# Indexer and attention scores of a hybrid decoder trunk: from fp32 to three fp32r passes, two head groups in turn on the two halves of the partitions

## The chip, the cores and the metric

The kernel runs on one core of a Trainium2 chip. The metric is the device time of one execution in microseconds. Five engines work side by side: TensorE (PE, with its weight loads listed as PEld), VectorE (DVE), ScalarE (ACT), GpSimd (POOL) and SyncE (SP), which here only issues DMAs.

## What is computed

Two layers of a causal decoder trunk on 256 tokens of width 1024. Each layer has a half-step SwiGLU, a mixer with three branches (sparse attention, causal pooling, a chunked state-space scan), a second half-step SwiGLU and an input embedding. The change touches only the sparse attention: an indexer of 8 heads of 64 picks 64 keys per query, and 8 heads of 64 attend to them.

```python
idx = jnp.einsum("bqh,bqhs->bqs", wi,
                 jax.nn.relu(jnp.einsum("bqhd,bsd->bqhs", qi, k_idx)))
idx = jnp.where(causal[None], idx.astype(jnp.float32), -jnp.inf)
_, sel = lax.top_k(idx, k_top)
...
logits = jnp.einsum("bqhr,bqkr->bqhk", ql, c_sel).astype(jnp.float32) * (HEAD_DIM ** -0.5)
probs = jax.nn.softmax(logits, axis=-1).astype(c_sel.dtype)
```

All inputs are float32. The kernel doesn't gather: it computes the scores of all keys from `q` and `kt` (the keys in head space) and adds a mask to those that weren't chosen.

## The kernel before

Activations lie with channels on the partitions and 256 tokens in the free dimension. Weights come from memory in units of 128x1024 (SP queue, `load`), and each unit is split: ACT rounds it to fp32r (`whi`, L128), DVE takes what is left (`wlo`, L129). A dense product is then three fp32r passes, high by high, high by low and low by high (`mm3`, L151 to L153), each a matmul of 128x128 weights over 256 columns. `AHEAD` lets two units be loaded beyond the one in use; four buffers stand for `raw`, `whi` and `wlo`.

The two products that the change touches were plain fp32. `indexer` (L636) and `attention` (L679) go over the queries in two blocks of 128 (h = 0 with 128 keys, h = 1 with 256 keys). Two heads share a chunk of 128 partitions: even heads on partitions 0 to 63, odd heads on 64 to 127. A group (`heads`) is four heads (h = 0) or two heads (h = 1) of the same parity, so that its scores fill one PSUM bank of 512 columns; all its matmuls have 64 rows, on the same half. A group's scores then go to ACT (relu, L639) and DVE (L646) in the indexer, or to DVE (L686), ACT (exp, L688), transposes (L697) and the product with the values (L711) in attention. An fp32 matmul is two matmul instructions, each with its own weight load; a transpose and an fp32r matmul are one.

`mix` runs the branches as generators, `weave` takes steps from them in turn, and a scheduler under the tile layer then sets the order on each engine by its own estimate of times. `choose` (the indexer) runs beside `silus` (convolution, gate and query projections), `attend` beside `states`, `pools` and `gate`. So bursts of a few score matmuls stand between long rows of `mm3` passes. There are eight PSUM banks, four tagged `mm` for the dense products and four tagged `aux` for everything else. The tag `a4` had four buffers of 4 KB a partition, taken in turn by the indexer's queries `qi`, the queries `q`, the keys `kt`, the values `vt` and the outputs of the scan.

Of the kernel before, what the change touches and what calls it, by code (L numbers as in the profile page):

```python
# [9 lines left out]
F = mybir.dt.float32  # L10
FR = mybir.dt.float32r
I32 = mybir.dt.int32
AF = mybir.ActivationFunctionType
OP = mybir.AluOpType
AX = mybir.AxisListType

P = 128
D = 1024
S = 256
# [45 lines left out]
class Builder:  # L65
# [191 lines left out]
    def constants(self):  # L257
        nc = self.nc
        c = self.const
        self.ident = c.tile([P, P], F, name="ident")  # L260
        self.ones = c.tile([P, P], F, name="ones")
        self.tri = c.tile([P, P], F, name="tri")
        self.up = c.tile([P, P], F, name="up")
        self.upr = c.tile([P, P], FR, name="upr")
        nc.gpsimd.memset(self.ones, 1.0)
        nc.gpsimd.affine_select(out=self.ident, in_=self.ones, pattern=[[-1, P]],
                                compare_op=OP.is_equal, fill=0.0, base=0, channel_multiplier=1)

        nc.gpsimd.affine_select(out=self.tri, in_=self.ones, pattern=[[1, P]],
                                compare_op=OP.is_ge, fill=0.0, base=0, channel_multiplier=-1)  # L270
        nc.gpsimd.affine_select(out=self.up, in_=self.ones, pattern=[[-1, P]],
                                compare_op=OP.is_gt, fill=0.0, base=0, channel_multiplier=1)
        nc.vector.tensor_copy(self.upr, self.up)
        self.onesr = c.tile([P, P], FR, name="onesr")
        nc.vector.tensor_copy(self.onesr, self.ones)

        warm = self.t([P, 1], tag="warm", bufs=1)
        nc.gpsimd.memset(warm, 0.0)
        nc.scalar.activation(warm, warm, AF.Tanh)
        self.cc = []  # L280
        for i in range(DEPTH):
            cc = c.tile([P, NCC], F, name=f"cc{i}")
            (nc.scalar, nc.gpsimd)[i].dma_start(cc, self.ins["cc"][i])
            self.cc.append(cc)

    def col(self, layer, name, i=0, n=1):
# [94 lines left out]
    def mix(self, layer, nxt):  # L381
        nc = self.nc
# [35 lines left out]
                                 accum_out=ss[:, 2 + h:3 + h])  # L418


        qi = self.a([P, 4, S], F, "a4", 4)
        for i in range(0, 4, 2):
            ps = self.in_pair(layer, T_QI + i, u0)
            self.later()
            nc.vector.tensor_tensor(qi[:, i:i + 2], ps, rb, op=OP.mult)


        self.uh = self.a([P, KD, S], FR, "uh", 2)
# [8 lines left out]


        xs = self.a([P, 8, S], F, "uh", 2)
        q = self.a([P, 4, S], F, "a4", 4)  # L440
        mb = [None, None]
        ki = self.a([P, S], F, "ki")
        ct = self.a([P, 2, 2, S], FR, "ct")

        def choose():
            v4 = self.t([P, 4], tag="v4", bufs=1)
            nc.vector.tensor_scalar(v4[:, :2], ss[:, :2], 1.0 / 256, EPS, op0=OP.mult, op1=OP.add)
            nc.vector.tensor_scalar(v4[:, 2:], ss[:, 2:], 1.0 / 64, EPS, op0=OP.mult, op1=OP.add)
            rk = self.t([P, 4], tag="rk", bufs=1)
            self.rsqrt(rk, v4, 4)  # L450
            for h in range(2):
                nc.vector.tensor_scalar(cn[:, h], cn[:, h], rk[:, h:h + 1], None, op0=OP.mult)
                nc.vector.tensor_scalar(ki2[:, h], sm[:, h, None, 8:72].to_broadcast([P, 2, 64]),
                                        rk[:, 2 + h:3 + h], None, op0=OP.mult)
            yield
            yield
            yield
            pk = self.bank("aux")
            for h in range(2):
                nc.tensor.transpose(pk[:, h * P:(h + 1) * P],  # L460
                                    ki2[:, h].rearrange("p a b -> p (a b)"), self.ident)
            nc.scalar.mul(ki, pk[:, :S], self.col(layer, "idx_k_norm"))
            yield
            yield
            mb[0] = yield from self.indexer(layer, 0, sm, qi, ki, idx[:, 0])
            pc = self.bank("aux")
            for c in range(2):
                for h in range(2):
                    nc.tensor.transpose(pc[:, c * S + h * P:c * S + (h + 1) * P],
                                        cn[:, h, c * P:(c + 1) * P], self.ident)  # L470
            for c in range(2):
                self.split_scaled(ct[:, 0, c], ct[:, 1, c], pc[:, c * S:(c + 1) * S],
                                  self.col(layer, "kv_norm", c))
            yield
            mb[1] = yield from self.indexer(layer, 1, sm, qi, ki, idx[:, 1])

        def silus():
# [12 lines left out]
            for i in range(0, 4, 2):  # L490
                ps = self.bank()
                yield from self.in_steps(layer, T_Q + i, u, ps)
                ps = ps.rearrange("p (a b) -> p a b", a=2)
                nc.scalar.mul(q[:, i:i + 2], ps, -0.125)


        def gates():
# [20 lines left out]
        res = {}  # L518

        def attend():  # L520
            kt = self.a([P, 4, S], F, "a4", 4)
            vt = self.a([P, 2, 512], F, "a4", 4)
            wk = self.unit(layer, U_KV, 1024)
            for i in range(0, 4, 2):
                ps = self.bank("aux")
                for j in range(2):
                    for c in range(2):
                        s = slice(c * 512 + (i + j) * P, c * 512 + (i + j + 1) * P)
                        self.mm3(ps[:, j * S:(j + 1) * S], (wk[0][:, s], wk[1][:, s]),
                                 (ct[:, 0, c], ct[:, 1, c]), c == 0, c == 1)  # L530
                nc.scalar.copy(kt[:, i:i + 2], ps.rearrange("p (a b) -> p a b", a=2))
                yield
            wv = self.unit(layer, U_KV + 1, 1024)
            for h in range(2):
# [84 lines left out]
    def heads(g, n):  # L619
# [2 lines left out]
        return ([g // 2 * 2 * n + 2 * j + odd for j in range(n)],  # L622
                slice(odd * 64, odd * 64 + 64))

    def indexer(self, layer, h, sm, qi, ki, idx):

        nc = self.nc
        nk = (h + 1) * P
        per = 512 // nk
        qs = slice(h * P, (h + 1) * P)  # L630
        for g in range(8 // per):
            heads, rows = self.heads(g, per)
            ps = self.bank("aux")
            for j, hd in enumerate(heads):
                c = hd // 2
                nc.tensor.matmul(ps[:, j * nk:(j + 1) * nk], qi[rows, c, qs], ki[rows, :nk],  # L636
                                 start=True, stop=True)
            t = self.t([P, 512])
            nc.scalar.activation(t, ps, AF.Relu)  # L639
            for j, hd in enumerate(heads):  # L640
# [24 lines left out]
    def attention(self, layer, h, mb, q, kt, vt, ya):  # L665
# [5 lines left out]
        qs = slice(h * P, (h + 1) * P)  # L671
        py = self.bank("aux")
        before = None
        for g in range(8 // per):
            heads, rows = self.heads(g, per)
            ps = self.bank("aux")
            for j, hd in enumerate(heads):
                c = hd // 2
                nc.tensor.matmul(ps[:, j * nk:(j + 1) * nk], q[rows, c, qs], kt[rows, c, :nk],  # L679
                                 start=True, stop=True)  # L680
            pr = self.t([P, per, nk])
            mx = self.t([P, per], tag="mx", bufs=2)
            sums = self.t([P, per], tag="sum", bufs=2)
# [34 lines left out]
    def ssd(self, layer, sm, xs, bc, cb, zs):  # L718
# [64 lines left out]
        for g in range(2):  # L783
# [50 lines left out]
            yield  # L834
            if g == 0:
                ysh, ysl = [], []
            ysh.append(self.a([P, 4, S], FR, "a4", 4))
            ysl.append(self.a([P, 4, S], FR, "a4", 4))
            for i in range(4):
                k = g * 4 + i  # L840
                nc.vector.tensor_tensor(y[:, k], y[:, k], zs[:, k], op=OP.mult)
# [228 lines left out]
def program(arrays):  # L1070

    order = None
    for last in (False, True):
        nc = bacc.Bacc("TRN2", target_bir_lowering=False, num_devices=1)
        ins = {k: nc.dram_tensor(f"in_{k}_dram", v.shape, F, kind="ExternalInput").ap()
               for k, v in arrays.items()}
        out = nc.dram_tensor("out_0_dram", (2, P, D), F, kind="ExternalOutput").ap()
# [13 lines left out]
```

## Time and profile before

| | us |
|---|---|
| median of 3 runs | 1355.15 (1353.79 to 1355.48) |
| the profiled execution, whole time | 1354.48 |
| its span, first to last instruction | 1352.8 |
| PE, weight loads, DVE, ACT busy in it | 1336.3, 1312.7, 1039.7, 745.0 |

Matmuls are pipelined: a matmul's listed duration (277 ns for 256 columns) is the time until its result stands, and the next one starts earlier than that. What a matmul costs in a row of matmuls is read from the distance of starts in the timeline. A row of the timeline merges neighbours of one line: it gives the start of the first, the time from there to the end of the last, and their count.

### The profile page before, as it was taken

How to read it: one execution, taken by the hardware profiler on the slowest of the kernel's cores; microseconds unless marked ns; L12 is line 12 of the kernel's file. 1: busy time of each engine (PE TensorE's matmuls, PEld its weight loads, DVE VectorE, ACT ScalarE, POOL GpSimd, SP SyncE). 2: the span in 40 equal slices, each digit the busy share in tenths (PEclk: the TensorE clock that was granted, in tenths of full speed). 3: DMA queues.
4: the chain of work that ended last, by engine and by line, in shares of the span. 5: the costliest groups of instructions: out<-in, count | busy, mean ns of one | idle time of the engine just before them, and what ended most of it. 6: DMA issues, size and time to landing. Idle time of an engine off the chain costs nothing.

```text
span 1352.8 us, 28288 instructions
## 1 busy us (share of the span) xinstructions
PE 1336.3 (99%) x11500; PEld 1312.7 (97%) x11500; DVE 1039.7 (77%) x1962; ACT 745.0 (55%) x1203; POOL 3.1 (0%) x14
## 2 busy tenths in 40 slices
PE   8999999999999999999999999999999999999997
PEld 7999999999899999999999999999989999999997
DVE  7777669877889787766887766797788887777666
ACT  5545456648654554544655444565576545545454
POOL 0000000000000000000000000000000000000000
PEclk9999999999999999999999999999999999999999
DMA  7666656554356666666566666565533666666661
GB/s 255 190 199 190 196 162 199 172 180 125 110 170 188 196 194 196 191 199 191 185 187 190 198 190 191 180 187 161 175 110 110 192 203 190 194 196 191 195 193 62
DMA packets 67714, 242.97 MB, mean 180 GB/s; under 512 B 7520, under 2 KB 7648, under 8 KB 67584
## 3 DMA queue, kind: packets, MB, share of 16 engines
q1 hardware_dynamic: 66816, 239.89, 57.3%
q8 instruction: 90, 1.47, 0.4%
q10 hardware_dynamic: 720, 1.16, 0.2%
q14 instruction: 40, 0.33, 0.1%
q0 software_dynamic: 48, 0.11, 0.0%
HBM read 240.09 MB, written 1.05 MB: 178 GB/s over the span
## 4 chain that ended last, share of the span: by engine, by line
PE 95%; DVE 3%; ACT 1%; issue 0%; DMA 0%; SPq 0%; DVEq 0%; ACTq 0%
PE mm L151 29%; PE mm L152 29%; PE mm L153 29%; DVE wlo L129 1%; PE aux L679 1%; PE aux L636 1%; PE aux L151 1%; PE aux L152 1%; PE aux L153 1%; PE aux L798 1%; PE aux L809 1%; PE aux L711 1%; PE aux L697 0%; ACT whi L128 0%; DMA h<-in_x_dram 0%
## 5 line engine op out<-in xcount | busy, mean ns | idle before, releaser
L128 ACT CAST whi<-raw 128x1024 fp32r<-128x1024 f32 (+1 forms) x457 | 476.4, 1045 | 507.6 <-issue 245.9
L151 PE MATMUL mm<-uh,whi 128*128 128x256 f32 x2560 | 713.3, 279 | 6.5 <-ACT whi L145 5.9
L129 DVE TENSOR_TENSOR wlo<-raw,whi 128x1024 fp32r<-128x1024 f32 (+1 forms) x457 | 554.5, 1215 | 214.0 <-ACT whi L128 210.8
L152 PE MATMUL mm<-ul,whi 128*128 128x256 f32 x2560 | 710.3, 278 | 0.2
L153 PE MATMUL mm<-uh,wlo 128*128 128x256 f32 x2560 | 709.4, 277 | 0.0
L151 PEld LDWEIGHTS mm<-uh,whi 128*128 128x128 f32 x2560 | 482.1, 188 | 13.2 <-ACT whi L145 5.9
L152 PEld LDWEIGHTS mm<-ul,whi 128*128 128x128 f32 x2560 | 482.4, 188 | 1.7 <-DVE ul L172 0.9
L153 PEld LDWEIGHTS mm<-uh,wlo 128*128 128x128 f32 x2560 | 482.2, 188 | 0.7 <-issue 0.3
L153 PE MATMUL mm<-gh,wlo 128*128 128x256 f32 x704 | 194.3, 276 | 0.0
L151 PE MATMUL mm<-gh,whi 128*128 128x256 f32 x704 | 194.3, 276 | 0.0
L152 PE MATMUL mm<-gl,whi 128*128 128x256 f32 x704 | 194.3, 276 | 0.0
L152 PEld LDWEIGHTS mm<-gl,whi 128*128 128x128 f32 x704 | 132.2, 188 | 0.0
L153 PEld LDWEIGHTS mm<-gh,wlo 128*128 128x128 f32 x704 | 132.2, 188 | 0.0
L151 PEld LDWEIGHTS mm<-gh,whi 128*128 128x128 f32 x704 | 132.2, 188 | 0.0
L151 PE MATMUL mm<-a,whi 128*128 128x256 f32 x256 | 70.9, 277 | 0.0
L152 PE MATMUL mm<-a,whi 128*128 128x256 f32 x256 | 70.7, 276 | 0.0
L153 PE MATMUL mm<-a,wlo 128*128 128x256 f32 x256 | 70.7, 276 | 0.0
L151 PEld LDWEIGHTS mm<-a,whi 128*128 128x128 f32 x256 | 48.1, 188 | 0.0
L153 PEld LDWEIGHTS mm<-a,wlo 128*128 128x128 f32 x256 | 48.1, 188 | 0.0
L152 PEld LDWEIGHTS mm<-a,whi 128*128 128x128 f32 x256 | 48.1, 188 | 0.0
L341 DVE TENSOR_TENSOR t<-mm,rs_r 128x256 f32<-128x256 f32 x88 | 37.3, 423 | 10.0
L171 ACT ACTIVATE uh<-h,cc 128x256 fp32r<-128x256 f32 x64 | 31.8, 504 | 18.7 <-DVE h L313 13.7
(214 smaller groups left out, 1142.0 us busy)
## 6 DMA issues: line engine op xcount, KB each, us to landing
raw<-in_w_dram SPq DMA_DIRECT2D x447, 512.0 KB, 3.8
raw<-in_w_dram SPq DMA_DIRECT2D x8, 352.0 KB, 3.0
raw<-in_w_dram SPq DMA_DIRECT2D x4, 256.0 KB, 3.5
h<-in_x_dram SPq DMA_DIRECT2D x2, 256.0 KB, 4.2
h<-in_x_dram SPq DMA_DIRECT2D x1, 512.0 KB, 6.3
t<-in_p_dram ACTq DMA_DIRECT2D x2, 256.0 KB, 5.2
out_dram<-uh SPq DMA_DIRECT2D x2, 256.0 KB, 2.8
out_dram<-uh ACTq DMA_DIRECT2D x2, 256.0 KB, 3.0
```

The source lines that it names most:

```text
L128: nc.scalar.copy(hi[:, :n], raw[:, :n])
L129: nc.vector.tensor_tensor(lo[:, :n], raw[:, :n], hi[:, :n].bitcast(F), op=OP.subtract)
L151: mm(ps, a[0], b[0], start=start, stop=False)
L152: mm(ps, a[0], b[1], start=False, stop=False)
L153: mm(ps, a[1], b[0], start=False, stop=stop)
L171: self.nc.scalar.mul(hi, src, scale)
L341: nc.vector.tensor_tensor(t, p1[0], r, op=OP.mult)
L636: nc.tensor.matmul(ps[:, j * nk:(j + 1) * nk], qi[rows, c, qs], ki[rows, :nk], start=True, stop=True)
L679: nc.tensor.matmul(ps[:, j * nk:(j + 1) * nk], q[rows, c, qs], kt[rows, c, :nk], start=True, stop=True)
L711: nc.tensor.matmul(py[o:o + 64, hd // 2 * P:(hd // 2 + 1) * P], vt[:, b, hd * 64:(hd + 1) * 64], x[:, j * nb + b], start=(b == 0), stop=(b ...
L798: nc.tensor.matmul(pl, self.upr, at[i].rearrange("p a b -> p (a b)"), start=(i == 0), stop=(i == 1))
L809: nc.tensor.matmul(ps[b:b + 64, k * P:(k + 1) * P], xt[:, h, h0 + j], m[:, j], start=True, stop=True)
```

## The change

The four operands `qi`, `ki`, `q` and `kt` are now kept in two fp32r parts, high and low, made by the helpers that split weights: `split` (ACT rounds, L167; DVE subtracts, L168) and `split_scaled` (L171, L172). For `qi` the product with the norm is first written to a scratch tile. `products` computes two groups of scores at once, an even and an odd one, into two `aux` banks: for each head three passes, and at each pass the even group's matmul (partitions 0 to 63) and the odd group's (64 to 127) stand next to each other. `a4` gets seven buffers and `ki` two; to make room the scratch for DMAs that GpSimd starts shrinks, and the second layer's constants `cc` are loaded from ACT's queue, where GpSimd loaded them.

```diff
-            (nc.scalar, nc.gpsimd)[i].dma_start(cc, self.ins["cc"][i])
+            nc.scalar.dma_start(cc, self.ins["cc"][i])
...
-        qi = self.a([P, 4, S], F, "a4", 4)
+        qi = [self.a([P, 4, S], FR, "a4", 7) for _ in range(2)]
...
-            nc.vector.tensor_tensor(qi[:, i:i + 2], ps, rb, op=OP.mult)
+            t = self.t([P, 2, S])
+            nc.vector.tensor_tensor(t, ps, rb, op=OP.mult)
+            self.split(qi[0][:, i:i + 2], qi[1][:, i:i + 2], t)
...
-            nc.scalar.mul(ki, pk[:, :S], self.col(layer, "idx_k_norm"))
+            self.split_scaled(ki[0], ki[1], pk[:, :S], self.col(layer, "idx_k_norm"))
...
-                nc.scalar.mul(q[:, i:i + 2], ps, -0.125)
+                self.split_scaled(q[0][:, i:i + 2], q[1][:, i:i + 2], ps, -0.125)
...
-                nc.scalar.copy(kt[:, i:i + 2], ps.rearrange("p (a b) -> p a b", a=2))
+                self.split(kt[0][:, i:i + 2], kt[1][:, i:i + 2],
+                           ps.rearrange("p (a b) -> p a b", a=2))
...
+    def products(self, g, per, qs, nk, q, key):
+
+
+        sides = [(self.bank("aux"), *self.heads(g + i, per)) for i in range(2)]
+        for j in range(per):
+            for x, y in ((0, 0), (1, 0), (0, 1)):
+                for ps, heads, rows in sides:
+                    c = heads[j] // 2
+                    self.nc.tensor.matmul(ps[:, j * nk:(j + 1) * nk], q[x][rows, c, qs],
+                                          key(y, c)[rows, :nk], start=(x + y == 0), stop=(y == 1))
+        return [(ps, heads) for ps, heads, _ in sides]
...
+        two = []
         for g in range(8 // per):
-            heads, rows = self.heads(g, per)
-            ps = self.bank("aux")
-            for j, hd in enumerate(heads):
-                c = hd // 2
-                nc.tensor.matmul(ps[:, j * nk:(j + 1) * nk], qi[rows, c, qs], ki[rows, :nk],
-                                 start=True, stop=True)
+            if g % 2 == 0:
+                two = self.products(g, per, qs, nk, qi, lambda y, c: ki[y])
+            ps, heads = two[g % 2]
...
-            for j, hd in enumerate(heads):
-                c = hd // 2
-                nc.tensor.matmul(ps[:, j * nk:(j + 1) * nk], q[rows, c, qs], kt[rows, c, :nk],
-                                 start=True, stop=True)
+            if g % 2 == 0:
+                two = self.products(g, per, qs, nk, q, lambda y, c: kt[y][:, c])
+            ps, heads = two[g % 2]
...
-        nc = bacc.Bacc("TRN2", target_bir_lowering=False, num_devices=1)
+        nc = bacc.Bacc("TRN2", target_bir_lowering=False, num_devices=1,
+                       dynamic_dma_scratch_size=1024)
```

Attention takes the same two lines as the indexer, and the outputs of the scan take `a4` with seven buffers.

What this does to the order on the engines, at three places. First PE in the first layer's indexer, h = 0. Before, the second of the two groups (an fp32 matmul stands as one row here; x4 are its four heads), with dense passes on both sides:

```order
L153 MATMUL mm_2977<-uh_2707,wlo_2908 128x256
L636 MATMUL aux_3008<-ki_2743,a_374_2582 128x128 x4
L151 MATMUL mm_2977<-uh_2707,whi_2943 128x256
L152 MATMUL mm_2977<-ul_2708,whi_2943 128x256
L153 MATMUL mm_2977<-uh_2707,wlo_2944 128x256
```

Now, the first of four heads of both groups (`a_374` and `a_375` are the parts of `qi`, `ki_2751` and `ki_2752` those of `ki`, the two `aux` are the two banks; L636 is a line of `products` now):

```order
L153 MATMUL mm_2795<-uh_2714,wlo_2883 128x256
L636 MATMUL aux_2976<-ki_2751,a_374_2582 128x128
L636 MATMUL aux_2977<-ki_2751,a_374_2582 128x128
L636 MATMUL aux_2976<-ki_2751,a_375_2583 128x128
L636 MATMUL aux_2977<-ki_2751,a_375_2583 128x128
L636 MATMUL aux_2976<-ki_2752,a_374_2582 128x128
L636 MATMUL aux_2977<-ki_2752,a_374_2582 128x128
```

Two bursts of 4 fp32 matmuls (8 instructions) have become one burst of 24 single instructions, which alternate between the halves.

Second, PE in the first layer's attention, h = 1. Before, the second group, cut in two by a matmul of the scan (L798), and one that follows:

```order
L153 MATMUL mm_4380<-uh_2707,wlo_4224 128x256
L679 MATMUL aux_4404<-a_549_3873,a_400_2742 128x256
L798 MATMUL aux_4360<-t_640_4356,upr 128x512
L679 MATMUL aux_4404<-a_549_3873,a_400_2742 128x256
L151 MATMUL mm_4380<-uh_2707,whi_4223 128x256
```

Now, the first pair of groups (L636 is the score matmul here too, and the scan's L798 has become L809):

```order
L153 MATMUL mm_4284<-uh_2714,wlo_4194 128x256
L809 MATMUL aux_4365<-t_629_4335,upr 128x512
L636 MATMUL aux_4374<-a_554_3917,a_403_2749 128x256
L636 MATMUL aux_4375<-a_554_3917,a_403_2749 128x256
L636 MATMUL aux_4374<-a_554_3917,a_404_2750 128x256
L809 MATMUL aux_4365<-t_630_4336,upr 128x512
L636 MATMUL aux_4375<-a_554_3917,a_404_2750 128x256
L636 MATMUL aux_4374<-a_555_3918,a_403_2749 128x256
```

One burst in each layer is still cut in two by a matmul of full height, before and now.

Third, DVE in the first layer where the indexer's queries are finished and the mixer's input is split. Before, up to the last piece of `ul`:

```order
L433 SCALAR_TENSOR_TENSOR t_398_2737<-h,cc_88,rs_r_2460 128x256
L425 TENSOR_TENSOR a_374_2582<-mm_2645,rs_r_2460 128x512
L447 TENSOR_SCALAR v_403_2745<-ss_2491 128x2
L448 TENSOR_SCALAR v_403_2745<-ss_2491 128x2
L129 TENSOR_TENSOR wlo_2770<-raw_2768,whi_2769 128x1024
L168 TENSOR_TENSOR ul_2708<-t_398_2737,uh_2707 128x256
```

Now (L426 is the old L425, L435 the old L433):

```order
L426 TENSOR_TENSOR t_391_2710<-mm_2649,rs_r_2460 128x512
L168 TENSOR_TENSOR ul_2715<-t_400_2740,uh_2714 128x256
L435 SCALAR_TENSOR_TENSOR t_401_2744<-h,cc_88,rs_r_2460 128x256
L449 TENSOR_SCALAR v_408_2754<-ss_2491 128x2
L168 TENSOR_TENSOR a_375_2583<-t_391_2710,a_374_2582 128x512
L168 TENSOR_TENSOR ul_2715<-t_401_2744,uh_2714 128x256
```

The subtraction for `qi` stands ahead of the last piece of `ul`, and the `wlo` that stood there now comes after it. A like subtraction for the first half of `qi` has been put in some rows earlier.

## Rows read from the trace of the kernel before

**Rows 1.** The page, part 1: busy time (share of span), instructions.

```profile
PE 1336.3 (99%) x11500; PEld 1312.7 (97%) x11500; DVE 1039.7 (77%) x1962; ACT 745.0 (55%) x1203; POOL 3.1 (0%) x14
```

**Rows 2.** The page, part 4: the chain that ended last, by engine.

```profile
PE 95%; DVE 3%; ACT 1%; issue 0%; DMA 0%; SPq 0%; DVEq 0%; ACTq 0%
```

**Rows 3.** Waits of PE, all but two: us in total, times, longest.

```profile
PE mm L151 <- ACT whi L145: 5.9, 1, 5.9
PE aux L245 <- DVE t L238: 0.9, 4, 0.3
```

**Rows 4.** Groups by line and form, PE: count; busy us, mean ns of one; idle.

```profile
L679 PE MATMUL aux<-a,a 64*128 64x256 f32 x32 | 9.6, 408 | 0.0
L636 PE MATMUL aux<-ki,a 64*128 64x256 f32 x32 | 9.0, 402 | 0.0
L679 PE MATMUL aux<-a,a 64*128 64x128 f32 x32 | 4.6, 285 | 0.0
L636 PE MATMUL aux<-ki,a 64*128 64x128 f32 x32 | 4.6, 285 | 0.0
```

**Rows 5.** Timeline of PE, a burst over 128 keys: start us, us, operation.

```profile
225.86 0.28 PE L153 MATMUL mm<-uh,wlo 128*128 128x256 f32 x1
...
226.20 0.28 PE L153 MATMUL mm<-uh,wlo 128*128 128x256 f32 x1
226.40 1.16 PE L636 MATMUL aux<-ki,a 64*128 64x128 f32 x8
...
228.19 0.28 PE L153 MATMUL mm<-uh,wlo 128*128 128x256 f32 x1
```

**Rows 6.** Timeline of PE, a burst over 256 keys.

```profile
257.90 0.28 PE L153 MATMUL mm<-uh,wlo 128*128 128x256 f32 x1
258.11 1.13 PE L636 MATMUL aux<-ki,a 64*128 64x256 f32 x4
...
259.96 0.28 PE L151 MATMUL mm<-uh,whi 128*128 128x256 f32 x1
```

**Rows 7.** Timeline of PEld and PE: eight instructions on one half, and on two.

```profile
226.40 0.96 PEld L636 LDWEIGHTS aux<-ki,a 64*128 64x128 f32 x8
...
323.58 0.42 PEld L809 LDWEIGHTS aux<-t,ul 128*64 128x64 f32 x8
...
323.58 0.66 PE L809 MATMUL aux<-t,ul 128*64 128x128 f32 x8
```

**Rows 8.** Timeline of PE, four matmuls of full height and one column.

```profile
402.80 0.28 PE L153 MATMUL mm<-a,wlo 128*128 128x256 f32 x1
402.92 0.50 PE L231 MATMUL aux<-ones,acc 128*128 128x1 f32 x4
...
403.95 0.28 PE L153 MATMUL mm<-a,wlo 128*128 128x256 f32 x1
```

**Rows 9.** Groups by line and form, DVE and ACT, of the operations that are added.

```profile
L168 DVE TENSOR_TENSOR a<-aux,a 128x512 fp32r<-128x512 f32 x4 | 2.8, 688 | 0.2
L172 DVE SCALAR_TENSOR_TENSOR ct<-aux,cc,ct 128x256 fp32r<-128x256 f32 x4 | 1.9, 474 | 0.0
L167 ACT CAST t<-t 128x512 fp32r<-128x512 f32 x2 | 1.2, 621 | 3.2 <-DMA t<-in_p_dram 3.2
```

**Rows 10.** Stages: length, then PE, PEld, DVE, ACT, POOL busy, clock, DMA.

```profile
205.00:216.00 11.00, 11.00 (x100) 11.00 (x99) 10.96 (x27) 6.27 (x12) 0.00 (x0) 1.00 0.57 185
...
176.00:375.00 199.00, 199.00 (x1647) 189.03 (x1647) 161.43 (x364) 125.40 (x235) 0.59 (x2) 1.00 0.50 155
```

**Rows 11.** Timeline of DVE where the mixer's input is split.

```profile
212.81 1.22 DVE L129 TENSOR_TENSOR wlo<-raw,whi 128x1024 fp32r<-128x1024 f32 x1
213.95 0.42 DVE L168 TENSOR_TENSOR ul<-t,uh 128x256 fp32r<-128x256 f32 x1
```

**Rows 12.** Timeline of ACT at the start: its queue, then its operations.

```profile
0.80 0.41 ACTq L283 DMA_DIRECT2D cc<-in_cc_dram  x1
...
4.24 0.91 ACT L171 ACTIVATE uh<-h,cc 128x256 fp32r<-128x256 f32 x2 [1.49 <-DMA cc<-in_cc_dram]
```

More of the change, by code (lines that the diff above doesn't have):

```diff
@@ L439, in mix @@
         xs = self.a([P, 8, S], F, "uh", 2)
-        q = self.a([P, 4, S], F, "a4", 4)
+        q = [self.a([P, 4, S], FR, "a4", 7) for _ in range(2)]
         mb = [None, None]
-        ki = self.a([P, S], F, "ki")
+        ki = [self.a([P, S], FR, "ki", 2) for _ in range(2)]
         ct = self.a([P, 2, 2, S], FR, "ct")
@@ L520, in attend @@
         def attend():
-            kt = self.a([P, 4, S], F, "a4", 4)
-            vt = self.a([P, 2, 512], F, "a4", 4)
+            kt = [self.a([P, 4, S], FR, "a4", 7) for _ in range(2)]
+            vt = self.a([P, 2, 512], F, "a4", 7)
             wk = self.unit(layer, U_KV, 1024)
@@ L673, in attention @@
         before = None
+        two = []
         for g in range(8 // per):
-            heads, rows = self.heads(g, per)
-            ps = self.bank("aux")
-            for j, hd in enumerate(heads):
-                c = hd // 2
-                nc.tensor.matmul(ps[:, j * nk:(j + 1) * nk], q[rows, c, qs], kt[rows, c, :nk],
-                                 start=True, stop=True)
+            if g % 2 == 0:
+                two = self.products(g, per, qs, nk, q, lambda y, c: kt[y][:, c])
+            ps, heads = two[g % 2]
             pr = self.t([P, per, nk])
@@ L836, in ssd @@
                 ysh, ysl = [], []
-            ysh.append(self.a([P, 4, S], FR, "a4", 4))
-            ysl.append(self.a([P, 4, S], FR, "a4", 4))
+            ysh.append(self.a([P, 4, S], FR, "a4", 7))
+            ysl.append(self.a([P, 4, S], FR, "a4", 7))
             for i in range(4):
```

## The prediction

> **What bounds the kernel now.** I read the page's busy times first, then its chain, then PE's waits, and last the timeline of PE. PE is listed as busy for 1336.3 of 1352.8 us, and its weight loads for 1312.7, where DVE has 77% and ACT 55% [rows 1]. The chain that ended last runs over PE for 95% of its length [rows 2]. PE's waits are the 5.9 us before its first matmul, 0.9 us at the norms [rows 3] and two more below a microsecond each. None of them lies in the indexer or in attention. So PE is never short of work, and a microsecond taken off PE's row of matmuls is a microsecond of the kernel, until something else is late.
>
> Since listed durations overlap, I measure by starts. Three dense passes take from 225.86 to 226.20 [rows 5], 0.113 us each. The score matmuls stand as bursts between such passes.
>
> **What the bursts cost now.** Over 128 keys: from the last dense pass at 226.20 to the one at 228.19 are 1.99 us. That stretch holds the burst and six dense passes (that at 226.20 and five behind the burst), 0.68 us, so the burst costs 1.31 us [rows 5]. Its eight instructions load weights every (0.96 - 0.19) / 7 = 0.11 us [rows 7], which makes 0.88. The other 0.43 is going in and out: 0.20 us instead of 0.113 before it, a slow first instruction, and slow passes behind it. Over 256 keys: 257.90 to 259.96 are 2.06 us with seven dense passes (0.79), so 1.27 us for four instructions [rows 6]. Less the same 0.43 that is 0.84, or 0.21 each: twice the columns, twice the time.
>
> The in and out belongs to the 64 rows, not to fp32. Four fp32 instructions of full height and one column stand in a stretch of 402.80 to 403.95, 1.15 us, with six dense passes (0.68) [rows 8]: 0.47 us, or 0.118 each, with nearly nothing on top. The same rows say that an instruction with a fresh load of 128 weight columns costs 0.11 to 0.12 us even when it has one column to compute.
>
> There are 32 instructions of each form in each function [rows 4]. By eight and by four that is 8 bursts over 128 keys and 16 over 256: 8 x 1.31 + 16 x 1.27 = 30.8 us of PE time in the kernel.
>
> **What they cost after the change.** Two groups share a burst, so there are 4 bursts of 24 instructions and 8 of 12. In and out: 12 x 0.43 = 5.2 us. That is half of what it was, whatever else happens. One burst per layer is cut in two by a matmul of full height, as before; this cancels. The 192 instructions cost 192 p, with p the time per instruction in the burst. So the change gives 30.8 - 5.2 - 192 p = 25.6 - 192 p, and it breaks even at p = 0.133 us. Everything hangs on p, which no row shows, as neighbours on different halves of the partitions don't occur in this trace.
>
> The bounds of p come from the nearest rows. The low end is two matmuls at a time. The scan's L809 matmuls write to two halves of the output partitions in turn, and there eight weight loads take 0.42 us in all where eight on one half take 0.96, and the eight matmuls are through in 0.66 [rows 7] where those on one half take 1.16 [rows 5]. These loads have 64 columns instead of 128, but two run side by side. At two at a time a pair would take 0.113, p = 0.056. The high end is going in and out of the row mode at each change of half, at the 0.20 us that a start after a change of height takes [rows 5], p = 0.206. Between them lies p = 0.113, one after another at the pace of a load. I take 0.056: the rows with alternating halves are nearer in kind than those that change the height of the array, for there the halves change at each instruction too. Gain: 25.6 - 192 x 0.056 = 14.9 us.
>
> The Trainium skill, "TensorE: Matmul & The Clock Gate", section "LDWEIGHTS (loading the stationary operand)", says that a load's time goes by its columns and not by its rows, which speaks against this gain. By that rule alone, with loads in turn, the sum would be that of p = 0.113; the loads of rows 7 do overlap, on another split of the array.
>
> **The other parts.** DVE gets, in two layers, 4 subtractions for `qi`, 4 for `q`, 4 for `kt` at 0.69 us and 2 for `ki` at 0.47 [rows 9]: 12 x 0.69 + 2 x 0.47 = 9.2 us. ACT gets 4 roundings of 0.62 [rows 9], 2.5 us; its other new forms replace copies of equal size. In 176 to 375 us, the first layer's mixer, DVE is idle for 199 - 161.4 = 37.6 us and ACT for 73.6 [rows 10]; against 4.6 and 1.2 us of new work per layer this cover holds on average. It is thin in one place: from 205 to 216 us DVE is busy for 10.96 of 11 us [rows 10], and PE waits there for the pieces of `ul`. Two new subtractions (1.4 us) go in ahead of the last piece, and one `wlo` of 1.22 us, which stood right before it [rows 11], goes behind it, so that piece comes at most 0.2 us later. I charge nothing. If the cover is gone, it is 1.4 us per layer, 2.8 in all. Behind `ki` and `kt` PE has dense passes queued. 48 of them stand between the transposes for `ki` and its first use, 5.4 us, against 0.47 for the subtraction and two or three queued operations of up to 1.22.
>
> The second bank of each pair is held until the first group's rows are through DVE. Attention then has its output bank, two score banks and one more of the four. Where the cover is short PE waits for a bank; no such wait is listed before. Bounds: 0 and, as an estimate, one `wlo` of 1.22 us [rows 11] at each of the 6 pairs of attention in the kernel, 7.3 us. I take 1 us, near the lower end, since the scheduler puts dense passes ahead of waiting matmuls, and the passes that it has for this are the same as before.
>
> The second `cc` on ACT's queue costs one issue of 0.41 us, behind the table load, where ACT then waits 1.49 us for the first `cc` [rows 12]: nothing; -0.3 to +0.4 us. Seven buffers for `a4` take away waits that PE doesn't have; new addresses change no instruction; both nothing.
>
> Sum against the profiled execution: 1354.48 - 14.9 + 1 = 1340.6 us. That execution is 0.67 us below the median of the runs, so I say 1341.
>
> **The rivals.** *One after another.* The halves don't overlap, and the change doesn't do what it says. p = 0.113 gives 25.6 - 21.7 = 3.9 us, all from fewer entries; with the 1 us and the 0.67, 1352.3. For it: two loads of 128 columns at a time are nowhere in the trace. Against it: the loads of L809.
>
> *Short passes cost like fp32.* An fp32r pass of 128 columns doesn't occur in the trace either. At what an fp32 matmul takes there, two instructions of 0.11, a pair takes 0.22 and p = 0.11 for half of the instructions, 0.056 for the rest: 10.6 + 5.4 = 16.0, gain 9.6 us; 1346.6 by the same sum.
>
> *A drain at each change of half* (the other side). In the bursts of `products` each instruction waits until the array is empty, p = 0.206: 25.6 - 39.6 = -14.0 us, 1370 by the same sum. It decides from p = 0.133 on. For it: each change of height shows this 0.20. Against it: L809 changes halves eight times without it.
>
> The Trainium skill, "TensorEngine Tiling (Array Packing)", section "Key Properties", says that changing the tiling mode drains the engine, and changing only the tile doesn't. By this rule the in and out of rows 5 and 6 stays and the last rival falls; rows 7 agree on the second half of it for columns, and none shows it for rows.
>
> **How the numbers follow.** My forecast gets 0.56, one after another 0.19, short passes 0.12, the drain 0.07, and 0.06 is left for new waits that take most of the gain. A measurement of this kernel can tell about 0.2% from no change, 2.7 us, so below 1352.4 is faster. The forecast, the short passes and half of the case of one after another are faster: 0.56 + 0.12 + 0.10 = 0.78, and 0.01 of the new waits makes 0.79. No change: the other half of that case and part of the new waits, 0.13. Slower: the drain and a little of the new waits, 0.08. The range goes from 1338 (no new wait, and a microsecond and a half more from passes behind the bursts) to 1353, a little past the 1352.3 of one after another; it leaves out the drain, the slow end of that case and most of the new waits.
>
> **What the profile after would show.** If I am right, a burst of 24 `aux` instructions over 128 keys lists loads in pairs a few ns apart and takes about 1.8 us net, one of 12 over 256 keys 1.1 us; PE's waits stay under 2 us in the mixers; DVE's busy time rises by 9 us. Loads evenly 0.11 us apart would be one after another; starts 0.2 us apart the drain; pairs 0.22 apart only over 128 keys the short passes. Waits of PE on DVE's `ki`, `ul` or on a bank in attention would make my 1 us wrong.

## The result and the profile after

The changed kernel takes 1344.8 us (median, 1344.17 to 1345.52) where the kernel before takes 1354.9 beside it: a ratio of 0.993, 95% interval 0.992 to 0.994, or 10.0 us less. The forecast was 1341, so the gain came out 4 us short. The profiled execution is the one of 1344.17 us, with a span of 1342.4. In a second measurement (e10 below) the ratio was 0.994 (0.993 to 0.996); one of its twelve executions ran at a granted clock of 0.947, the others at 0.997 to 0.998, and took 1360.2 us, and without it the ratio is 0.993.

The page after, part 1, to set against [rows 1]:

```profile
PE 1323.2 (99%) x11564; PEld 1304.8 (97%) x11564; DVE 1046.5 (78%) x1976; ACT 745.0 (55%) x1207; POOL 2.4 (0%) x13
```

And part 4, the chain by engine, to set against [rows 2]:

```profile
PE 88%; DVE 9%; issue 1%; ACT 1%; DMA 0%; DVEq 0%; POOL 0%; ACTq 0%; POOLq 0%
```

PE lost 13 us of busy time with 64 instructions more. But the chain now runs over DVE for 9% of its length where it was 3%, so DVE has begun to set the time somewhere. PE's waits (us in total, times, longest) say where, beside those of [rows 3]:

```profile
PE mm L151 <- ACT whi L145: 6.1, 1, 6.1
PE mm L153 <- DVE wlo L129: 2.1, 4, 1.4
PE aux L245 <- DVE t L238: 1.2, 4, 0.6
```

The second row is new: dense passes wait for `wlo`.

**The bursts.** The timeline of PE (start us, us, operation) at a burst over 128 keys and one over 256 keys, to set against [rows 5] and [rows 6]. L636 is now the line of all score products, in `products`:

```profile
224.93 0.28 PE L153 MATMUL mm<-uh,wlo 128*128 128x256 f32 x1
225.13 1.55 PE L636 MATMUL aux<-ki,a 64*128 64x128 f32 x24
...
227.07 0.28 PE L151 MATMUL mm<-uh,whi 128*128 128x256 f32 x1
...
258.39 0.28 PE L153 MATMUL mm<-uh,wlo 128*128 128x256 f32 x1
258.60 0.98 PE L636 MATMUL aux<-ki,a 64*128 64x256 f32 x12
...
259.95 0.28 PE L151 MATMUL mm<-uh,whi 128*128 128x256 f32 x1
```

By the prediction's own reckoning the first stretch is 2.14 us with four dense passes (0.45), net 1.69; the second is 1.56 us with four, net 1.11. The forecast was 1.8 and 1.1. Matmul by matmul, the two of a pair start at most 5 ns apart in these bursts. From the second pair on, a pair starts 0.112 us behind the one before it over 128 keys and 0.119 us over 256, so p = 0.056 and 0.059. What is left of the net time, 0.35 and 0.40 us, is the way in and out.

**Where the gain stands.** The 10,848 dense passes come in the same order in all kernels, but for 36 (28 in e2) that change places inside attention's stages, so the start of the n-th one can be compared between traces at the bounds of the stages. The table takes passes 1561, 2281, 3101 (which bound the indexer's stage and attention's in layer 1) and 6961, 7681, 8701 (layer 2); before, they start at 188.84, 282.12, 410.03, 851.64, 944.95 and 1095.58 us. Each entry is how much longer (+) or shorter (-) the stage became against before; "start" is what stood at pass 1561 already.

| | start | indexer 1 | attention 1 | indexer 2 | attention 2 | the four |
|---|---|---|---|---|---|---|
| changed | -1.62 | -0.73 | -2.85 | -2.33 | -2.97 | -8.9 |
| changed, again (e10) | +0.19 | -0.77 | -2.77 | -2.35 | -2.95 | -8.8 |
| e1 | -0.48 | -3.87 | -2.41 | -3.85 | -2.44 | -12.6 |
| e2 | -1.59 | +0.65 | +1.93 | +0.59 | +1.75 | +4.9 |
| e3 | -1.41 | -0.93 | -2.79 | -1.09 | -2.91 | -7.7 |
| e4 | -1.15 | +0.42 | -1.69 | -1.42 | -1.73 | -4.4 |
| e5 | -1.28 | -3.45 | -2.55 | -3.43 | -2.91 | -12.3 |
| e7 | -0.93 | +1.23 | -2.82 | -0.99 | -2.91 | -5.5 |
| e9 | -0.61 | -3.85 | -2.80 | -3.80 | -2.91 | -13.4 |

In the indexer's stage of one layer the bursts alone are worth 3.8 us: two of 1.31 and four of 1.27 before (7.7), one of 1.69 and two of 1.11 after (3.9). The changed kernel keeps 0.7 of that in layer 1 and 2.3 in layer 2. That is what the experiments are about.

What stood ahead of pass 1561 and behind pass 8701 is no part of these stages; both profiles of the changed kernel are 0.3 us longer behind.

**What PE waits for there.** First the timeline of ACT of the changed kernel in layer 1, behind the indexer's first burst (in brackets: idle before it, and what ended it):

```profile
231.58 0.51 ACT L619 ACTIVATE gh<-t,cc 128x256 f32<-128x256 f32 x1 [1.65 <-DVE t L616]
232.00 1.07 ACT L652 ACTIVATE t<-aux 128x512 f32<-128x512 f32 x2
```

Then DVE's, where L657 and L659 are the eight multiply-adds and L670 begins the selection:

```profile
229.97 1.52 DVE L616 SCALAR_TENSOR_TENSOR t<-mm,cc,t 128x255 f32<-128x255 f32 x3 [1.00 <-ACT t L614]
232.61 0.29 DVE L657 TENSOR_SCALAR gl<-t,sm 128x128 f32<-128x128 f32 x1 [1.13 <-ACT t L652]
232.94 2.75 DVE L659 SCALAR_TENSOR_TENSOR gl<-t,sm,gl 128x128 f32<-128x128 f32 x7
236.14 0.29 DVE L670 MAX8 m<-gl 128x8 f32<-128x128 f32 x1 [0.46 <-POOL gl L663]
...
236.74 1.22 DVE L129 TENSOR_TENSOR wlo<-raw,whi 128x1024 fp32r<-128x1024 f32 x1
```

And PE's:

```profile
236.37 0.28 PE L152 MATMUL mm<-ul,whi 128*128 128x256 f32 x1
238.01 0.39 PE L153 MATMUL mm<-uh,wlo 128*128 128x256 f32 x1 [1.37 <-DVE wlo L129]
```

The burst was over at 226.6, but ACT's order has both relus (L652) behind a silu (L619) that waits for DVE until 231.6, so DVE stands idle for 1.13 us. Then all eight multiply-adds and the first selection step run in a row, and the `wlo` that PE needs comes behind them. PE starts nothing from 236.4 to 238.0. In the kernel before, the two relus (L639 there) ran 4 us apart, and DVE did a `wlo` between the fourth multiply-add and the fifth (L646):

```profile
227.66 0.58 ACT L639 ACTIVATE t<-aux 128x512 f32<-128x512 f32 x1
...
231.65 0.60 ACT L639 ACTIVATE t<-aux 128x512 f32<-128x512 f32 x1
```

```profile
229.70 1.11 DVE L646 SCALAR_TENSOR_TENSOR gl<-t,sm,gl 128x128 f32<-128x128 f32 x3
...
232.22 1.22 DVE L129 TENSOR_TENSOR wlo<-raw,whi 128x1024 fp32r<-128x1024 f32 x1
233.35 1.51 DVE L646 SCALAR_TENSOR_TENSOR gl<-t,sm,gl 128x128 f32<-128x128 f32 x4
```

Layer 2 of the changed kernel has the same eight in a row (892.9 to 896.0 us), but no wait as long as this one: between the burst over 128 keys and the first over 256 it loses 1.1 us in shorter stretches, where layer 1 loses 2.7.

### The profile page after: what moved, and what is told of

It reads as the page before. It is cut to its first block, busy times and chain, and to the rows that moved or that the text cites. A ratio compares the mean times of both kernels' runs of the same rounds, so it can differ in the third digit from the quotient of the medians.

```text
span 1342.4 us, 28442 instructions
## 1 busy us (share of the span) xinstructions
PE 1323.2 (99%) x11564; PEld 1304.8 (97%) x11564; DVE 1046.5 (78%) x1976; ACT 745.0 (55%) x1207; POOL 2.4 (0%) x13
## 3 DMA queue, kind: packets, MB, share of 16 engines
q10 hardware_dynamic: 864, 1.28, 0.3%
## 4 chain that ended last, share of the span: by engine, by line
PE 88%; DVE 9%; issue 1%; ACT 1%; DMA 0%; DVEq 0%; POOL 0%; ACTq 0%; POOLq 0%
PE mm L153 27%; PE mm L151 27%; PE mm L152 27%; DVE wlo L129 3%; PE aux L636 1%; DVE t L616 1%; PE aux L151 1%; PE aux L820 1%; PE aux L152 1%; PE aux L153 1%; PE aux L809 1%; PE aux L722 1%; PE aux L708 0%; DVE t L435 0%; DVE ul L168 0%
## 5 line engine op out<-in xcount | busy, mean ns | idle before, releaser
L153 PE MATMUL mm<-uh,wlo 128*128 128x256 f32 x2560 | 710.6, 278 | 2.3 <-DVE wlo L129 2.1
L153 PEld LDWEIGHTS mm<-uh,wlo 128*128 128x128 f32 x2560 | 481.3, 188 | 5.2 <-DVE wlo L129 3.9
L153 PE MATMUL mm<-gh,wlo 128*128 128x256 f32 x704 | 194.5, 276 | 0.0
L153 PEld LDWEIGHTS mm<-gh,wlo 128*128 128x128 f32 x704 | 132.2, 188 | 0.0
L153 PE MATMUL mm<-a,wlo 128*128 128x256 f32 x256 | 70.8, 277 | 0.0
L153 PEld LDWEIGHTS mm<-a,wlo 128*128 128x128 f32 x256 | 48.1, 188 | 0.0
L171 ACT ACTIVATE uh<-h,cc 128x256 fp32r<-128x256 f32 x64 | 31.8, 504 | 18.2 <-DVE h L313 13.7
```

The source lines that it names most:

```text
L153: mm(ps, a[1], b[0], start=False, stop=stop)
L171: self.nc.scalar.mul(hi, src, scale)
```

## The experiments

**The theory:** the bursts pay what was forecast, and about 4 us of it are given back in the indexer's stage by the order of ACT and DVE there. **The rivals:** the subtractions that the change adds on DVE cost this time wherever they stand; or pairing as such costs it, by banks held longer and scores that come late. The start of the kernel is one more suspect.

### e1: fp32 operands, two groups in turn

```diff
+    def products(self, g, per, qs, nk, q, key):
+        sides = [(self.bank("aux"), *self.heads(g + i, per)) for i in range(2)]
+        for j in range(per):
+            for ps, heads, rows in sides:
+                c = heads[j] // 2
+                self.nc.tensor.matmul(ps[:, j * nk:(j + 1) * nk], q[rows, c, qs],
+                                      key(c)[rows, :nk], start=True, stop=True)
...
-            heads, rows = self.heads(g, per)
-            ps = self.bank("aux")
...
+            if g % 2 == 0:
+                two = self.products(g, per, qs, nk, qi, lambda c: ki)
+            ps, heads = two[g % 2]
```

> The kernel before with one edit: operands stay whole in fp32, one instruction of the program per head, but the products of two groups (even and odd heads) are issued in turn on the two halves, so 24 bursts become 12. Nothing is added on VectorE or ScalarE. TensorE's sum: before 8 bursts of 1.31 us and 16 of 1.27 us = 30.8 us; here, if halves overlap as they do in the changed kernel, 4 of 1.31 and 8 of 1.27 = 15.4 us, a gain of 15.4 us in the bursts. What is given back tells the theories apart. Theory (the changed kernel gives 6 to 7 us back because VectorE's order in the indexer's first half puts eight multiply-adds in a row ahead of a wlo; here a wlo stands among them again in layer 1): 1339 to 1342 us. Rival 1 (the subtractions added on VectorE take the time back): the same, 1339 to 1342. Rival 2 (pairing itself takes it back, through two banks held at once and late scores): 1345 to 1347, no better than the changed kernel. Rival 3 (fp32 operands don't overlap on the two halves): 12 bursts of 0.43 and 192 halves in series as before = 1350 us.

Measured: 1342.5 us, ratio 0.991 (0.990 to 0.993), half a microsecond above the theory's band and no slower than the changed kernel. The burst over 128 keys holds 16 instructions, two for each of eight heads:

```profile
225.70 0.28 PE L153 MATMUL mm<-uh,wlo 128*128 128x256 f32 x1
225.91 1.16 PE L631 MATMUL aux<-ki,a 64*128 64x128 f32 x16
...
227.46 0.29 PE L151 MATMUL mm<-uh,whi 128*128 128x256 f32 x1
```

Net 1.31 us (1.76 less four passes), what 8 instructions cost before. So fp32 matmuls overlap on the two halves too, and turns alone bring the gain: three fp32r passes were not needed for it. The indexer's stage shortens by 3.87 and 3.85 us, all that the bursts are worth. Pairing as such costs nothing there; that rival falls. The other stays, since e1 adds no subtraction. In attention, where the changed kernel gains 2.9 us a layer, e1 gains only 2.4.

### e2: two parts and three passes, groups not paired

```diff
-            if g % 2 == 0:
-                two = self.products(g, per, qs, nk, qi, lambda y, c: ki[y])
-            ps, heads = two[g % 2]
...
+            for j, hd in enumerate(heads):
+                c = hd // 2
+                for x, y in ((0, 0), (1, 0), (0, 1)):
+                    nc.tensor.matmul(ps[:, j * nk:(j + 1) * nk], qi[x][rows, c, qs],
+                                     ki[y][rows, :nk], start=(x + y == 0), stop=(y == 1))
```

> The changed kernel without the turns: operands in two parts, three fp32r passes, and all the added splits, but each group is issued by itself where it stood before, 24 bursts on one half each. TensorE: 24 x 0.43 us + 192 passes of 0.113 us = 32.0 us, 1.2 us more than before. Theory (VectorE's order is what costs, and the added subtractions by themselves nearly nothing): 1354.9 + 1.2 + 0 to 1 = 1355 to 1357 us. Rival 1 (the added subtractions cost 5 us or more): 1360 to 1363 us.

Measured: 1358.9 us, ratio 1.003 (1.002 to 1.004), between the two. In the indexer's stage it is as the theory has it: +0.65 and +0.59, of which 0.36 is a wait near 213 us (below) and the rest the bursts. The miss is in attention, +1.9 and +1.8, where the scheduler's order differs again. One transpose waits for its exponentials, in the trace as

```profile
328.00 0.28 PE L153 MATMUL mm<-uh,wlo 128*128 128x256 f32 x1
328.78 0.33 PE L704 MATMUL aux<-ident,t 128*128 128x128 f32 x1 [0.50 <-ACT t L699]
```

0.78 us from start to start in place of 0.11. That explains part of it; the rest is not separated and stays open.

### e3: the indexer's steps placed earlier

```diff
-        self.weave((choose(), 26), (silus(), 60), (some(12), 12))
+        self.weave((choose(), 34), (silus(), 60), (some(12), 12))
```

> The changed kernel with one number changed: the steps of the indexer are spread over the projections' steps by a count of 34 in place of 26. The scheduler then puts a wlo and the convolutions among the multiply-adds of the first half in layer 1 (three multiply-adds, a wlo, then single ones between convolutions) where eight stood together. Same instructions, same bursts. Theory (order on VectorE): 3 to 5 us of the 6 to 7 come back, 1340 to 1342 us, and the wait of 1.5 us for wlo near 236 us is gone. Rival 1 (amount of VectorE work, not its order): unchanged, 1344 to 1346 us. Rival 2 (banks held by pairs): unchanged or slower, since the pairs come earlier.

Measured: 1345.3 us, ratio 0.994 (0.992 to 0.995): nothing gained, which spoke against the theory. PE's waits:

```profile
PE mm L153 <- DVE wlo L129: 1.9, 5, 0.4
PE aux L462 <- DVE ki L455: 1.4, 2, 0.7
```

The long wait for `wlo` is gone as expected, but five short ones stand in its place, and the transposes for `ki` now come before DVE has made it: the number moves the whole indexer against the dense passes, not only eight instructions. The edit was too coarse to tell order from amount, and e5 does it by hand.

### e4: one half after the other

```diff
-        for j in range(per):
-            for x, y in ((0, 0), (1, 0), (0, 1)):
-                for ps, heads, rows in sides:
+        for ps, heads, rows in sides:
+            for j in range(per):
+                for x, y in ((0, 0), (1, 0), (0, 1)):
```

> The changed kernel with the loops of the paired products turned inside out: all passes of the even group first, then all of the odd group, in the same 12 bursts. Same instructions, same VectorE work. Theory (the pace is halved only by taking turns): 192 passes of 0.113 us in place of 0.056 to 0.059, 192 x 0.055 = +10.6 us, 1355 to 1356 us. Rival (the halves don't need turns, queueing ahead is enough): 1345 us.

Measured: 1349.3 us, ratio 0.996 (0.995 to 0.998), 4.5 us slower than the changed kernel and not 10.6. A burst of 12 over 256 keys:

```profile
259.33 0.28 PE L153 MATMUL mm<-uh,wlo 128*128 128x256 f32 x1
259.53 1.32 PE L636 MATMUL aux<-ki,a 64*128 64x256 f32 x12
...
261.12 0.28 PE L153 MATMUL mm<-uh,wlo 128*128 128x256 f32 x1
```

Net 1.79 - 3 x 0.113 = 1.45 us, where 12 in series would take 0.43 + 12 x 0.113 = 1.79 net. In the program all six passes of the even group stand ahead of the odd group's. In the trace the odd group's first pass starts at 259.88, while three of the even group's six are still to start; those run in pairs. Over 128 keys it is three of twelve, and the burst is 2.66 us net against 1.69 in turns. So turns decide, but PE reaches some passes ahead across the halves by itself. Both answers that I wrote down were too simple.

### e5: the changed kernel with e1's order

```diff
+            if h == 0 and g == 0:
+                for x in self.silus[-2:]:
+                    self.first_then(r, x)
...
+            if h == 0 and g == 1:
+                for m, x in zip((3, 4, 5), self.convs[-3:]):
+                    self.first_then(ms[m], x)
```

`r` is the relu, `ms` the multiply-adds, `silus` and `convs` the silus and convolution steps recorded so far; `first_then(a, b)` only tells the scheduler that b stands behind a on their engine. The edit names no `wlo`; the scheduler put one ahead of the eighth multiply-add by itself, in both layers.

> The changed kernel with the order of the indexer's first half put by hand as it stands in e1: on ScalarE the first relu ahead of the two silus that stand before it in the changed kernel, on VectorE the last three multiply-adds of the first group and the first of the second in turn with convolutions, and a wlo ahead of the eighth, in both layers. Same instructions, same 12 bursts, all the added subtractions still there. The landmarks give what is lost in the indexer's stage of the changed kernel, against its bursts: 3.1 us in layer 1 and 1.5 in layer 2, of which 0.35 each at the dense passes that wait for ul near 213 us. Theory A (the order: late relus and eight multiply-adds ahead of a wlo): all but the 0.35 each comes back, 3.8 us, 1341 us. Theory B (the amount: each added subtraction on a nearly full VectorE is paid, wherever it stands): nothing comes back, 1344 to 1345 us; and then e2, where only the amount is added, is the explained one.

Measured: 1341.9 us, ratio 0.990 (0.989 to 0.992); theory A said 1341, B 1344 to 1345. The indexer's stage gives -3.45 and -3.43, in both layers alike. The timeline of DVE there (in this kernel L668 is the multiply-add, L617 the convolution, L130 makes `wlo`):

```profile
230.66 1.13 DVE L668 SCALAR_TENSOR_TENSOR gl<-t,sm,gl 128x128 f32<-128x128 f32 x3
231.70 0.48 DVE L617 SCALAR_TENSOR_TENSOR t<-mm,cc,t 128x255 f32<-128x255 f32 x1
...
233.66 1.22 DVE L130 TENSOR_TENSOR wlo<-raw,whi 128x1024 fp32r<-128x1024 f32 x1
234.79 0.35 DVE L668 SCALAR_TENSOR_TENSOR gl<-t,sm,gl 128x128 f32<-128x128 f32 x1
```

And what is left of PE's waits for `wlo`:

```profile
PE mm L154 <- DVE wlo L130: 0.2, 1, 0.2
```

All added subtractions are still there, and DVE is busy nearly as long (1044.8 us for 1046.5). In the indexer's stages 3.8 us came back: outside the bursts no dense pass there loses over 0.1 us any more, but for the place near 213 us (below). Of the whole time it is 2.7 us, each kernel taken against before on its own chip; attention in layer 1 gives 0.3 back, where PE waits once for an exponential (L720). So it was the order, not the amount. Two orders were put right at once, the relu's on ACT and the multiply-adds' on DVE; which of them counts for more is not separated.

### e6 and e9: indexer in fp32, attention in two parts, both in turn

The edit of e1 in the indexer, the change's own in attention; `qi` and `ki` aren't split.

> Indexer with whole fp32 operands in turn on the halves (as in e1, no splits of qi and ki), attention in two parts and three passes in turn (as in the changed kernel). By landmarks e1's indexer gains 3.85 us per layer and the changed kernel's attention 2.9 us per layer, against 2.4 for e1's attention. If the stages add: 2 x 6.75 = 13.5 us and up to 1 us from the start, 1340 to 1341 us. Rival (the splits of q, which stand at the end of the indexer's stage, and of kt cost there what qi's cost earlier): 1342 to 1344 us.

> The kernel of e6 once more, for its profile and beside the changed kernel on one chip. Expected 1340.7 to 1341.7 us; by landmarks -3.85 us per layer in the indexer's stage (no wait for wlo, no wait for ul near 213 us) and -2.9 in attention's. If the splits of q cost at the end of the indexer's stage, -3.4 there.

Measured: 1341.2 us, ratio 0.990 (0.988 to 0.991), and again 1340.3 us, 0.990 (0.988 to 0.991), beside 1346.0 for the changed kernel on that chip. The stages add up as expected: e1's gain in the indexer with the changed kernel's in attention. The chain on e9's page is that of before again:

```profile
PE 95%; DVE 3%; ACT 1%; issue 0%; DMA 0%; SPq 0%; DVEq 0%; ACTq 0%
```

Among PE's waits none for `wlo` or `ul` is left; the longest are:

```profile
PE mm L151 <- ACT whi L145: 6.1, 1, 6.1
PE aux L245 <- DVE t L238: 0.9, 4, 0.3
PE mm L151 <- ACT uh L171: 0.9, 2, 0.5
```

This is the fastest version: 14 us below before, and 5.7 below the changed kernel on the same chip.

### e7: qi's low part on GpSimd

```diff
-            self.split(qi[0][:, i:i + 2], qi[1][:, i:i + 2], t)
+            nc.scalar.copy(qi[0][:, i:i + 2], t)
+            nc.gpsimd.tensor_tensor(qi[1][:, i:i + 2], t, qi[0][:, i:i + 2].bitcast(F), op=OP.subtract)
```

> The changed kernel with the two subtractions per layer that make qi's low part (0.85 us each on VectorE) moved to GpSimd, which is busy for 2.4 us of the span. Order elsewhere as in the changed kernel: the eight multiply-adds stay together. Theory A (order): only the 0.35 us per layer at ul near 213 us comes back, 1344 us. Theory B (amount): 1.7 us per layer comes back, 1341 to 1342 us. Rival (GpSimd is slow or takes VectorE's access to memory): qi's low part later than 226 us or slower VectorE around 210 us, 1346 us or more.

(The 0.85 us in that text should be 0.69 [rows 9].) Measured: 1348.2 us, ratio 0.995 (0.994 to 0.996), 3 us slower than the changed kernel: the rival. The timeline of GpSimd, its two subtractions in layer 1:

```profile
206.81 1.64 POOL L428 TENSOR_TENSOR a<-t,a 128x512 fp32r<-128x512 f32 x1 [204.91 <-ACT a L427]
213.66 2.03 POOL L428 TENSOR_TENSOR a<-t,a 128x512 fp32r<-128x512 f32 x1 [5.21 <-ACT a L427]
```

And of DVE meanwhile:

```profile
207.21 2.52 DVE L168 TENSOR_TENSOR ul<-t,uh 128x256 fp32r<-128x256 f32 x4
...
214.46 1.26 DVE L180 TENSOR_SCALAR rs_t<-v 128x4 int32<-128x4 int32 x1
```

In the changed kernel the four `ul` pieces take 1.43 us and the tiny L180 0.17. DVE lost 1.1 us each time, more than the 0.69 that it was spared. The second time L180 ends at 215.72, just behind GpSimd's 215.69. The run says nothing on order against amount.

### e8: the start alone

```diff
-            (nc.scalar, nc.gpsimd)[i].dma_start(cc, self.ins["cc"][i])
+            nc.scalar.dma_start(cc, self.ins["cc"][i])
...
```

The smaller scratch for GpSimd's DMAs goes with it, as in the change.

> The kernel before with the edit at the start alone: the second layer's constants cc are loaded over ScalarE's queue in place of GpSimd's, and the room for GpSimd's descriptors is cut. Indexer and attention stay as before. In the profiles so far the dense passes reach their full pace at 15.1 us in the kernel before and 13.7 in e1, which load one cc over GpSimd, and at 11.7 to 13.4 us in the six that load both over ScalarE; by the 120th dense pass those six stand 0.9 to 1.6 us ahead of before, e1 0.5. If the edit does that: 1353.0 to 1353.8 us, 0.9 to 1.4 less than before on the same chip. If it is chance from run to run: within 0.4 us of before.

Measured: 1354.1 us beside 1354.6, ratio 0.9993 (0.9985 to 1.0002), an interval that holds no change. At the 120th dense pass it stands 0.6 us ahead of before.

### e10: the changed kernel once more

> The changed kernel itself, on the same chip as e9: 1344.3 to 1345.3 us, and by landmarks less in layer 1's indexer than in layer 2's (-0.7 and -2.3 us in the first profile). If that gap between the layers was chance, both come out alike here.

Measured: 1346.0 us, ratio 0.994 (0.993 to 0.996), a little above what I wrote. The four stages repeat to 0.1 us, the difference between the layers included, and so does the long wait:

```profile
PE mm L153 <- DVE wlo L129: 1.4, 1, 1.4
```

What differs is the start: -1.62 us in the first profile, +0.19 here, with the same program. The timeline of PE shows where. In the first profile:

```profile
8.88 0.42 PE L153 MATMUL mm<-uh,wlo 128*128 128x256 f32 x1
...
9.90 0.28 PE L153 MATMUL mm<-uh,wlo 128*128 128x256 f32 x1
```

And in e10:

```profile
15.20 0.41 PE L153 MATMUL mm<-uh,wlo 128*128 128x256 f32 x1
...
15.78 0.28 PE L153 MATMUL mm<-uh,wlo 128*128 128x256 f32 x1
```

Dense passes start mostly 0.21 us apart until the granted clock goes from its lower level (1.2 GHz) to its upper (2.4 GHz), and 0.113 us apart from there on. In the first profile that is at 9.5 us, though waits for `ul` and `wlo` then take up part of what it gives; in e10 it is at 15.7 us, and in the profile of before at 15.1. So the 1.6 us that the first profile gains before 25 us come with the clock, and since the same program has it early once and late once, not with the edit to `cc`. Whether it goes by the execution or by the chip isn't separated. Of the 10.0 us that were measured first a part may be just that.

## Why the prediction was right, and where it was off

*The pace of a pair* was the term on which all hung, and it held: p = 0.056 over 128 keys and 0.059 over 256, net 1.69 and 1.11 us a burst for 1.8 and 1.1. In and out of the 64 rows took 0.35 and 0.40 us for the 0.43 forecast. The rivals one after another, short passes and drain fall with the same rows, and e4 shows what the kernel does when turns are taken away. The Trainium skill, "TensorEngine Tiling (Array Packing)", section "Key Properties", adds that different tiles can load and multiply in parallel; the loads and matmuls of the two halves, which start at most 5 ns apart in the two bursts shown, agree.

*The sum.* 14.9 us were forecast for the bursts, and the four stages gave 8.9, in e10 8.8. Of the 6.0 missing (the indexer's bursts by themselves gave 0.15 more than forecast):

- **3.8 us: DVE's and ACT's order in the indexer** (e5 against the changed kernel: 2.7 in layer 1, 1.1 in layer 2). This is the step that failed. I had counted the added work against DVE's idle time as an average over the mixer [rows 10] and looked for PE's waits on `ki`, `ul` and banks. I had not looked at what stands in a row on DVE once two groups' scores arrive together and the scheduler sets their relus behind another wait. The "1 us for new waits" was the term that should have held it, and its upper bound was for attention's banks, where no wait came.
- **0.7 us: the thin place.** I had said that it costs nothing since the last `ul` comes 0.2 us later at most. `ul` wasn't late. Late was the `wlo` that I had seen go behind it, whose own reader I didn't ask for. DVE of the changed kernel:

```profile
212.32 0.42 DVE L168 TENSOR_TENSOR ul<-t,uh 128x256 fp32r<-128x256 f32 x1
...
212.73 1.22 DVE L129 TENSOR_TENSOR wlo<-raw,whi 128x1024 fp32r<-128x1024 f32 x1
```

  And PE:

```profile
213.69 0.28 PE L152 MATMUL mm<-ul,whi 128*128 128x256 f32 x1
214.00 0.39 PE L153 MATMUL mm<-uh,wlo 128*128 128x256 f32 x1
```

  The `wlo` ends at 213.95 and L153 starts at 214.00, 0.31 us behind the pass ahead of it; with the slow start that follows, the stretch costs 0.35 us a layer. It appears in e2, e3, e4, e5 and both runs of the changed kernel, and not in e1 and e9, which don't split `qi`.
- **1.6 us: attention's bursts were worth 2.9 us a layer, not 3.7.** I had read the way in and out in the indexer, between dense passes [rows 5, 6], and charged it to attention's bursts as well. Taking each matmul's time as the distance to the next start, layer 1's products lose 3.10 us in the indexer (6.40 to 3.30, in e5) and 2.99 in attention (6.59 to 3.60, in the changed kernel). But the dense passes around them lose another 0.67 in the indexer (85.64 to 84.97 us for 720, in e9, where PE waits for nothing); in attention they lose 0.10 (99.04 to 98.94 for 820), and the scan's L809 (L798 before) and the value products of L722 (L711) take 0.34 and 0.30 longer, while the transposes take 0.35 less. There the bursts stand among other short matmuls, and entries that a pair saves are seen again beside those. That reading is argued from these sums; no run separates it.

The parts that were put at nothing: the start gave 1.6 us in the first profile and took 0.2 in e10, so that the first measurement came out only 4 us short is in part luck; no run shows a cost of `cc` (e8), `ki` and `kt` kept their cover, and no wait for a bank is listed. DVE's busy time rose by 6.8 us, not 9.2.

## What to carry to other kernels

Matmuls of 64 rows that stand alone on one half of the partitions are worth pairing with their neighbour on the other half, in turns and in the precision that they have; splitting them into cheaper passes is a second question. Here it only added work in the indexer, and in attention three fp32r passes in turn gained 0.4 to 0.5 us a layer over fp32 in turn (e9 against e1), which is why the mixed version is the fastest. When a change makes two producers finish together, look at the consumers' order on the busy engine and ask which of the main stream's small pieces now stands behind the heap; a share of idle time over the stage doesn't tell. And whoever sees an instruction pass behind another should ask who reads that instruction, not only who reads the one that got ahead.

## What the runs showed of the hardware

- fp32 matmuls (two instructions each) on alternating halves go through in pairs at the same pace as one alone: 16 instructions net 1.31 us where 8 took 1.31.
- Without turns the second half's first pass starts at 259.88, ahead of the first half's last three; the last of those starts at 260.23 (e4), though the program has it earlier. In this run starts on different halves don't keep the program's order.
- A GpSimd subtraction of 128x512 is listed with 1.64 to 2.03 us (0.69 on DVE), and a DVE instruction beside it is stretched by 1.1 us each time, even one of 128x4 (e7). The Trainium skill, "SBUF — State Buffer", section "Who interferes with whom", says that the two share a pair of ports and that the one that has them blocks the other for a whole instruction; the L180 that ends with GpSimd's subtraction agrees.
- The first 25 us of the same program differ by 1.8 us between two profiled executions, as much as a fifth of the effect under study. The granted clock rose at 9.5 us in one and at 15.7 in the other (e10).
